# Value products of the last key block in one strided instruction, one softmax scaling on ScalarE, and five operations moved: a hybrid encoder layer on Trainium2

## The chip, the cores and the metric

The kernel runs on one core of one Trainium2 chip. The metric is the device time of one execution in microseconds (us). The engines are TensorE (PE: products; PEld: its weight loads), VectorE (DVE), ScalarE (ACT), GpSimd (POOL) and SyncE (SP), which issues most of the transfers; every engine works through its own instructions in order and waits on semaphores for the others.

## The reference, cut to what matters

One encoder layer over 512 positions of width 1024, all in float32:

```python
h = layer_norm(x, ln0_g, ln0_b)
mix = hybrid_mixer(h, ...)
h = layer_norm(DN_ALPHA * h + mix, ln1_g, ln1_b)
h = layer_norm(DN_ALPHA * h + sq_relu_mlp(h, w_ff1, w_ff2), ln2_g, ln2_b)

# hybrid_mixer(u):
proj = u @ w_in            # q, k, v | z, x, B, C, dt | two gates
ya = neighbourhood_attention(q, k, v, rpb) @ w_attn_br
ys = ...                   # two-way Mamba-2 SSD in 8 groups, gated norm, @ w_ssd_br
merged = gates[:, :, 0] * ya + gates[:, :, 1] * ys
return merged @ w_o
```

The neighbourhood attention sees the 512 positions as a grid of 8 rows by 64 columns. Each query looks at all 8 rows and at 16 columns around its own, with a bias by relative position: `softmax(q k' / 8 + bias) v` for 16 heads of width 64.

## The kernel before

**Products in parts.** A float32 product is made of three products of rounded parts: high by high, low by high, high by low (`mm3`, L398 to L401). The high part of a weight slab is a rounding copy on ScalarE (L381, or L504 in the planned stages), the low part a subtraction on VectorE or GpSimd (L382, L508). Products accumulate in PSUM banks that are shared by tags: `mm` 2, `tr` 2, `so` 2, `yd` 1, `cb` 1.

**Stages, in order of time.** First norm and first projections (to about 46 us), the eight SSD groups (to about 500 us), the projection of the values (L1179 to L1194), the attention of 16 heads in 8 pairs (L1217 to L1333), its output projection `ps_abr` (L1348 to L1379), the gates and the merge (L1402 to L1414), `w_o`, the two feed-forward products, and at the very end the last quarter of the second one with the last norm (L1720 to L1741).

**What sets the order.** Up to the end of the SSD groups the order is a list: the first operations stand in a table, `HEAD` (L72 to L103), the others come from `Plan.order`, which simulates the engines with the cost of each operation; `Plan.issue` (L341 to L349) issues them as they are listed. Everything behind that is ordered by the tile framework, which simulates the engines' time, and where an edit changes a cost or a dependence there, instructions of all engines move. `behind(a, b)` and `after=` add a dependence of order.

**Places the change touches.** (1) In the chain for `dts` (softplus of the step widths) ScalarE copies `dtT` (L671), takes an absolute value (L683), an Exp (L684) and a second Exp for `ea` (L685); the Exp table is loaded before the first Exp. (2) In SSD group g, chunk c, a decay matrix `bc{g}_{c}` arrives by a transfer; VectorE subtracts (L958), selects (L962), ScalarE takes the Exp (L964), VectorE multiplies by the chunk's `cb` (L966), and TensorE uses it for the diagonal products `yd` (L972). Four reductions of the diagonal of `cb` (L882, two instructions each) lie between. (3) GpSimd multiplies a gate by the SSD result `ysacc` (L1409), twice for each of four blocks of columns. (4) For one head the scores of 4 query blocks m against 256 keys each lie in `sc` (128 x 4 x 256). VectorE adds the bias and takes the maximum (L1279), ScalarE takes the Exp with sums (L1285), VectorE the reciprocal of the sums (L1287) and four scalings (L1289). TensorE transposes eight blocks of 128 columns (`tp_p`, L1300), ScalarE copies the high parts `pth` (L1304), VectorE subtracts the low parts `ptl` (L1305), and TensorE multiplies the values by them into `po` (L1313, L1314, bank `yd`, one for all heads). Key block b serves the two query blocks b and b+1 modulo 4: for b = 0, 1, 2 they lie side by side in `po` and one product has 256 columns; for b = 3 they are blocks 3 and 0, and each has a product of 128 columns. ScalarE then copies one half of `po` (`low`, L1324) and VectorE adds both into `aT` (L1327). (5) The split of the second weight slab of the output projection, `wh_abr1`, is held behind the last `aTh` (L1352). (6) In the last loop (L1720) each block of 128 positions gets two products of 512 columns, each followed by an addition (L1727) and statistics (L1728).

Of the kernel before, what the change touches and what calls it, by code (L numbers as in the profile page):

```python
# [19 lines left out]
P = 128  # L20
S = 512
D = 1024
# [69 lines left out]
T:ps_dt.1 T:ps_dt.1 T:ps_dt.1 T:ps_x0_2.0 A:dtT.0 T:ps_x0_3.0 T:ps_x0_3.0 T:tp_dt.0  # L92
T:ps_x0_0.0 D:dts.0 T:ps_x0_1.0 T:ps_x0_1.0 A:dts.1 T:ps_x0_0.1 A:dts.1 T:ps_x0_1.1
T:ps_x0_1.1 T:ps_x0_0.1 T:ps_x0_0.1 T:ps_x0_0.1 A:ea.0 D:dts.2 T:ps_x0_2.0 D:dts.2
# [9 lines left out]
ON = {x[2:]: x[0] for x in HEAD}  # L104


class Plan:
# [233 lines left out]
    def issue(self):  # L341
        order = self.order(NUDGES)
        named = {}
        for o in self.ops:
            named.setdefault(".".join(map(str, o["w"][0])), []).append(o["i"])
        head = [named[x[2:]].pop(0) for x in HEAD]
        done = set(head)
        for i in head + [i for i in order if i not in done]:
            self.ops[i]["fn"]()  # L349
# [3 lines left out]
def encoder_layer(ctx, tc, x, w_in, w_attn_br, w_ssd_br, w_o, w_ff1, w_ff2, pcols, rows64,  # L353
# [825 lines left out]
    for s in range(2):  # L1179
# [9 lines left out]
        for b in range(4):  # L1189
            pv4 = pss[b].rearrange("p (r h q) -> p r h q", r=4, h=2)  # L1190
            hi = vhl[s][:, b, :, 0:4:3, :]
            nc.scalar.activation(hi, pv4, AF.Copy)
            nc.vector.tensor_tensor(out=vhl[s][:, b, :, 1:3, :], in0=pv4, in1=hi.bitcast(F32),
                                    op=ALU.subtract)  # L1194
# [22 lines left out]
    for pr in range(NH // 2):  # L1217
# [25 lines left out]
        for hh in range(2):  # L1243
# [44 lines left out]
            for m in range(4):  # L1288
                nc.vector.tensor_scalar(out=sc[:, m, :], in0=sc[:, m, :], scalar1=sums[:, m : m + 1],  # L1289
                                        scalar2=None, op0=ALU.mult)  # L1290

            pts = []
            for b2 in range(2):
                tp = psx.tile([P, 2, 2, P], F32, tag="tr", bufs=BANKS["tr"], name=f"tp_p{h}_{b2}")
                for j in range(2):
                    b = 2 * b2 + j
                    for which in range(2):
                        m = (b + which) % 4
                        half = (0 if b == 0 else 1) if m == 0 else 1 - which
                        nc.tensor.transpose(tp[:, j, which, :],  # L1300
                                            sc[:, m, half * P : (half + 1) * P], ident)
                pth = atp.tile([P, 2, 2, P], F32R, tag="pth", bufs=3, name=f"pth{h}_{b2}")
                ptl = atp.tile([P, 2, 2, P], F32R, tag="ptl", bufs=3, name=f"ptl{h}_{b2}")
                nc.scalar.activation(pth, tp, AF.Copy)  # L1304
# [5 lines left out]
            def pv(b, w0, nw, m0, start, stop):  # L1310
                th, tl = (t[:, b % 2, w0 : w0 + nw, :] for t in pts[b // 2])
                v = vhl[pr // 4][:, b, pr % 4, 2 * hh : 2 * hh + 2, :]
                nc.tensor.matmul(po[:, m0 : m0 + nw, :], v, th, start=start, stop=False)  # L1313
                return nc.tensor.matmul(po[:, m0 : m0 + nw, :], v, tl, start=False, stop=stop)  # L1314


            pv(0, 0, 2, 0, True, False)
            pv(2, 0, 2, 2, False, False)
            pv(1, 0, 2, 1, False, False)
            pv(3, 0, 1, 3, False, False)  # L1320
            last = pv(3, 1, 1, 0, False, True)
# [27 lines left out]
    for d2 in range(4):  # L1349
        wa = weights([(w_attn_br, 0, d2 * 256, 256)], KD, 256, f"abr{d2}",  # L1350
                     nc.vector if d2 else nc.gpsimd,
                     after=(ins.ins, ins.ins) if d2 == 1 else None)  # L1352
# [49 lines left out]
    for d2 in range(4):  # L1402
# [3 lines left out]
        for j in range(2):  # L1406
            d = 2 * d2 + j
            g0, g1 = ga[:, j, :], gs[:, j, :]
            nc.gpsimd.tensor_tensor(out=g1, in0=g1, in1=ysacc[:, d, :], op=ALU.mult)  # L1409
# [310 lines left out]
    for t in range(NT):  # L1720
        st = ffp.tile([P, 2, 6], F32, tag="ln2_st", bufs=2, name=f"ln2_st{t}")
        for i, slab in enumerate(slabs):
            ps = psx.tile([P, 512], F32, tag="mm", bufs=BANKS["mm"], name=f"ps_f2_3_{t}_{i}")
            for k0, w2 in zip((0, 4), slab):
                ff2(ps, t, *w2, k0)
            cs = slice(i * 512, (i + 1) * 512)
            nc.vector.tensor_tensor(out=acc[t][:, cs], in0=ps, in1=acc[t][:, cs], op=ALU.add)  # L1727
            nc.vector.bn_stats(st[:, i, :], acc[t][:, cs])  # L1728
# [7 lines left out]

        ends = (0, 512, 768, D) if t == NT - 1 else (0, 512, D)
# [65 lines left out]
```

## Time and profile before

| | us |
|---|---|
| median of 3 runs | 1187.24 (1186.92 to 1188.7) |
| profiled execution, its own time | 1186.48 |
| span of the profiled execution | 1184.7 |
| TensorE busy | 1158.4 |
| VectorE busy | 757.0 |
| ScalarE busy | 614.7 |
| GpSimd busy | 546.6 |

The mean granted TensorE clock was 0.997 of full speed. Rows of a timeline give start, duration, engine, line, operation, output and inputs, shapes and the number of equal instructions in a row; in brackets stands how long the engine had been idle and what ended that. Matmuls are pipelined: their own durations overlap, and the time that one takes of TensorE is read from its start to the next start. A list of waits gives the time in total, how often, and the longest.

### The profile page before, as it was taken

The page shows a single profiled execution, that of the slowest core. Times are in us where ns is not written, and L with a number is a line of the kernel's source. Part 1 is how long each engine was busy: PE and PEld are TensorE (multiplying, and loading weights), DVE is VectorE, ACT ScalarE, POOL GpSimd, SP SyncE. Part 2 cuts the span into 40 slices and gives each one's busy share as a digit, 9 for nine tenths or more (in the row PEclk, how much of TensorE's full clock was granted, in tenths as well). Part 3 has the DMA queues.
Part 4 walks back from the last instruction along what each step waited for, and adds up shares of the span by engine and source line. Part 5 has one row for each costly group of instructions (what it writes and reads, how often), then busy time and mean ns, then how long its engine had stood idle before and what let it go on. Part 6 is the DMA issues. An engine that isn't in the chain of part 4 may idle for free.

```text
span 1184.7 us, 16407 instructions
## 1 busy us (share of the span) xinstructions
PE 1158.4 (98%) x6114; PEld 988.1 (83%) x6114; DVE 757.0 (64%) x1361; ACT 614.7 (52%) x1033; POOL 546.6 (46%) x588
## 2 busy tenths in 40 slices
PE   5999999999999999999999999999999999999997
PEld 5988798989888888788888887888888888878885
DVE  7747475666657656443789975556543557488855
ACT  6676583837354654423667864342353555365410
POOL 1268968777788776403567541016046131222000
PEclk9999999999999999999999999999999999999999
DMA  6343333333333331333333223444236977788511
GB/s 201 105 150 124 105 127 107 116 112 129 104 110 107 125 124 54 107 106 85 86 86 86 57 69 107 156 147 144 87 107 181 240 195 199 184 212 226 167 50 54
DMA packets 129407, 149.19 MB, mean 126 GB/s; under 512 B 22960, under 2 KB 101808, under 8 KB 129328
## 3 DMA queue, kind: packets, MB, share of 16 engines
q1 hardware_dynamic: 115696, 112.63, 30.9%
q0 software_dynamic: 13056, 34.61, 12.0%
q8 instruction: 48, 0.79, 0.3%
q10 hardware_dynamic: 576, 0.92, 0.2%
q14 instruction: 31, 0.25, 0.1%
HBM read 145.90 MB, written 2.23 MB: 125 GB/s over the span
## 4 chain that ended last, share of the span: by engine, by line
PE 90%; DVE 3%; DMA 3%; issue 1%; ACT 1%; POOL 1%; DVEq 0%; SPq 0%; POOLq 0%; ACTq 0%
PE ps_f L399 8%; PE ps_f L401 8%; PE ps_f L400 8%; PE ps_x L401 5%; PE ps_x L399 5%; PE ps_x L400 5%; PE ps_abr L1363 3%; PE ps_g L399 2%; PE ps_g L401 2%; PE ps_g L400 2%; PE ps_z L399 2%; PE ps_sbr L399 2%; PE ps_z L400 2%; PE ps_z L401 2%; PE ps_sbr L401 2%; PE yd L972 2%
## 5 line engine op out<-in xcount | busy, mean ns | idle before, releaser
L779 DVE SCALAR_TENSOR_TENSOR cv<-ps_x,pc,cv 128x511 f32<-128x511 f32 (+1 forms) x128 | 95.7, 748 | 24.9 <-ACT cv L771 21.3
L400 PE MATMUL ps_f<-h1Th,wl_f 128*128 128x512 f32 (+1 forms) x288 | 104.0, 365 | 0.0
L399 PE MATMUL ps_f<-h1Th,wh_f 128*128 128x512 f32 (+1 forms) x288 | 103.7, 365 | 0.0
L401 PE MATMUL ps_f<-h1Tl,wh_f 128*128 128x512 f32 (+1 forms) x288 | 102.0, 365 | 0.0
L1564 DVE TENSOR_TENSOR wl_f<-w2r,wh_f 128x1024 fp32r<-128x1024 f32 x42 | 50.0, 1221 | 62.9 <-ACT wh_f L1563 62.6
L399 PE MATMUL ps_z<-wh_z,hTh 128*128 128x256 f32 x256 | 75.2, 294 | 1.0 <-DVE cv L779 1.0
L401 PE MATMUL ps_z<-wl_z,hTh 128*128 128x256 f32 x256 | 71.5, 279 | 0.0
L400 PE MATMUL ps_z<-wh_z,hTl 128*128 128x256 f32 x256 | 71.5, 279 | 0.0
L1558 POOL DMA_DIRECT2D w2r<-in_w_ff x30 | 36.3, 1421 | 71.7 <-DMA w2r<-in_w_ff 46.6
L400 PE MATMUL ps_f<-wh_f,sql 128*128 128x512 f32 x168 | 65.3, 390 | 0.3 <-DVE sql L1564 0.3
L1563 ACT ACTIVATE wh_f<-w2r 128x1024 fp32r<-128x1024 f32 x42 | 42.7, 1053 | 43.6 <-DMA w2r<-in_w_ff 33.5
L401 PE MATMUL ps_f<-wl_f,sqh 128*128 128x512 f32 x168 | 65.2, 390 | 0.1
L399 PE MATMUL ps_f<-wh_f,sqh 128*128 128x512 f32 x168 | 64.9, 389 | 0.0
L1094 DVE TENSOR_TENSOR ysacc<-ps_sbr,ysacc 128x512 f32<-128x512 f32 x56 | 38.4, 689 | 39.2 <-PE ps_sbr L401 39.0
L399 PEld LDWEIGHTS ps_f<-h1Th,wh_f 128*128 128x128 f32 x288 | 53.9, 188 | 9.1 <-ACT rl L1665 0.2
L400 PEld LDWEIGHTS ps_f<-h1Th,wl_f 128*128 128x128 f32 x288 | 53.9, 188 | 8.7
L382 DVE TENSOR_TENSOR wl_f<-ws_f,wh_f 128x1024 fp32r<-128x1024 f32 x36 | 47.2, 1348 | 20.7 <-ACT wh_f L381 20.5
L401 PEld LDWEIGHTS ps_f<-h1Tl,wh_f 128*128 128x128 f32 x288 | 52.8, 188 | 8.7
L1409 POOL TENSOR_TENSOR gt<-gt,ysacc 128x512 f32<-128x512 f32 x8 | 13.1, 1651 | 99.2 <-ACT gt L1112 91.1
L399 PE MATMUL ps_sbr<-yTh,wh_sbr 128*128 128x512 f32 x128 | 55.5, 434 | 1.1 <-DVE ysacc L1094 0.6
L399 PE MATMUL ps_x<-hTh,wh_bc 128*128 128x512 f32 (+1 forms) x144 | 56.6, 393 | 0.0
L401 PE MATMUL ps_x<-hTl,wh_bc 128*128 128x512 f32 (+1 forms) x144 | 53.6, 372 | 1.8 <-DVE hTl L621 1.8
(344 smaller groups left out, 3766.2 us busy)
## 6 DMA issues: line engine op xcount, KB each, us to landing
ws_f<-in_w_ff SPq DMA_DIRECT2D x20, 1024.0 KB
w2r<-in_w_ff POOLq DMA_DIRECT2D x18, 1024.0 KB, 7.5
bc<-acs_d SPq DMA_DIRECT2D x32, 512.0 KB
w2r<-in_w_ff POOLq DMA_DIRECT2D x30, 512.0 KB, 9.1
ws_bc<-in_w_in SPq DMA_DIRECT2D x16, 512.0 KB
ws_x<-in_w_in SPq DMA_DIRECT2D x8, 1024.0 KB
ws_z<-in_w_in SPq DMA_DIRECT2D x8, 1024.0 KB
ws_g<-in_w_in SPq DMA_DIRECT2D x8, 1024.0 KB
```

The lines of the kernel that those rows point to most:

```text
L382: (eng[i] if isinstance(eng, tuple) else eng).tensor_tensor(out=lo[:, k], in0=st[:, k], in1=hi[:, k].bitcast(F32), op=ALU.subtract)
L399: nc.tensor.matmul(o, lh, rh, start=start, stop=False)
L400: nc.tensor.matmul(o, ll, rh, start=False, stop=False)
L401: return nc.tensor.matmul(o, lh, rl, start=False, stop=stop)
L779: op("DVE", 0.75, lambda j=j, o=o, n=n: nc.vector.scalar_tensor_tensor(out=acc()[:, o], in0=ps()[:, n], scalar=tap(j), in1=acc()[:, o], op ...
L972: nc.tensor.matmul(yd()[:, c % 2, h * HD : (h + 1) * HD], bc()[:, 1, h, :], xtok()[:, c, h * HD : (h + 1) * HD], start=True, stop=True)
L1094: op("DVE", 0.69, lambda d=d, ps=ps: nc.vector.tensor_tensor(out=ysacc[:, d, :], in0=ps(), in1=ysacc[:, d, :], op=ALU.add), r=[(ps.name, 0 ...
L1363: ins.append(nc.tensor.matmul(pss[j], u, v, start=k + p == 0, stop=k == KD - 1 and p == 2))
L1409: nc.gpsimd.tensor_tensor(out=g1, in0=g1, in1=ysacc[:, d, :], op=ALU.mult)
L1558: nc.gpsimd.dma_start(t, rows(i, n, c, k), accum_op=ALU.add)
L1563: nc.scalar.activation(hi[:, k], x, AF.Copy)
L1564: low = nc.vector.tensor_tensor(out=lo[:, k], in0=x, in1=hi[:, k].bitcast(F32), op=ALU.subtract)
```

## The change

Six edits. (a) In the table of the first operations the Exp for `ea`, and the table load with it, goes ahead of the copy `dtT`. (b) The product of `bc0_3` by `cb` goes ahead of the subtraction for `bc0_2`. (c) GpSimd's first two gate products wait for the last eviction of the values. (d) The scaling of query block 0 goes to ScalarE; the transposes of key block 3 are stored in swapped order, and its products become one per part, with 256 columns that go to blocks 0 and 3 of `po`. (e) The split of `wh_abr1` waits for the last `pth` instead of the last `aTh`. (f) The second 512 columns of the last block of positions are done in two halves.

```diff
-T:ps_dt.1 T:ps_dt.1 T:ps_dt.1 T:ps_x0_2.0 A:dtT.0 T:ps_x0_3.0 T:ps_x0_3.0 T:tp_dt.0
...
+T:ps_dt.1 T:ps_dt.1 T:ps_dt.1 T:ps_x0_2.0 A:ea.0 A:dtT.0 T:ps_x0_3.0 T:ps_x0_3.0
...
+MOVE = (("bc0_3.1", 2), ("bc0_2.0", 1))
...
+        early, late = (named[x][n] for x, n in MOVE)
         head = [named[x[2:]].pop(0) for x in HEAD]
+        order.remove(early)
+        order.insert(order.index(late), early)
...
-            nc.scalar.activation(hi, pv4, AF.Copy)
+            vdone = nc.scalar.activation(hi, pv4, AF.Copy)
...
             for m in range(4):
-                nc.vector.tensor_scalar(out=sc[:, m, :], in0=sc[:, m, :], scalar1=sums[:, m : m + 1],
-                                        scalar2=None, op0=ALU.mult)
+                if m == 0:
+                    nc.scalar.activation(sc[:, m, :], sc[:, m, :], AF.Copy, scale=sums[:, m : m + 1])
+                else:
+                    nc.vector.tensor_scalar(out=sc[:, m, :], in0=sc[:, m, :],
+                                            scalar1=sums[:, m : m + 1], scalar2=None, op0=ALU.mult)
...
-                        nc.tensor.transpose(tp[:, j, which, :],
+                        nc.tensor.transpose(tp[:, j, 1 - which if b == 3 else which, :],
...
-                nc.scalar.activation(pth, tp, AF.Copy)
+                high_t = nc.scalar.activation(pth, tp, AF.Copy)
...
-            def pv(b, w0, nw, m0, start, stop):
-                th, tl = (t[:, b % 2, w0 : w0 + nw, :] for t in pts[b // 2])
+            for i, (b, ms) in enumerate(((0, slice(0, 2)), (2, slice(2, 4)), (1, slice(1, 3)),
+                                         (3, slice(0, 4, 3)))):
                 v = vhl[pr // 4][:, b, pr % 4, 2 * hh : 2 * hh + 2, :]
-                nc.tensor.matmul(po[:, m0 : m0 + nw, :], v, th, start=start, stop=False)
-                return nc.tensor.matmul(po[:, m0 : m0 + nw, :], v, tl, start=False, stop=stop)
-            pv(0, 0, 2, 0, True, False)
-            pv(2, 0, 2, 2, False, False)
-            pv(1, 0, 2, 1, False, False)
-            pv(3, 0, 1, 3, False, False)
-            last = pv(3, 1, 1, 0, False, True)
+                for j, t in enumerate(pts[b // 2]):
+                    last = nc.tensor.matmul(po[:, ms, :], v, t[:, b % 2], start=i + j == 0,
+                                            stop=i == 3 and j == 1)
...
-                     after=(ins.ins, ins.ins) if d2 == 1 else None)
+                     after=(high_t.ins, high_t.ins) if d2 == 1 else None)
...
-            nc.gpsimd.tensor_tensor(out=g1, in0=g1, in1=ysacc[:, d, :], op=ALU.mult)
+            gy = nc.gpsimd.tensor_tensor(out=g1, in0=g1, in1=ysacc[:, d, :], op=ALU.mult)
+            if d2 == 0:
+                behind(gy, vdone, "the values")
...
+        ends = (0, 512, 768, D) if t == NT - 1 else (0, 512, D)
...
+        for i, (c0, c1) in enumerate(zip(ends, ends[1:])):
+            ps = psx.tile([P, c1 - c0], F32, tag="mm", bufs=BANKS["mm"], name=f"ps_f2_3_{t}_{i}")
...
+                ff2(ps, t, w2[0][:, :, cs], w2[1][:, :, cs], k0)
+            nc.vector.tensor_tensor(out=acc[t][:, c0:c1], in0=ps, in1=acc[t][:, c0:c1], op=ALU.add)
+            nc.vector.bn_stats(st[:, i, :], acc[t][:, c0:c1])
```

What that moves, at three places. In the listings a line number is that of the kernel listed, and a number behind a name tells one buffer from another.

VectorE in the first SSD group, around the chunks 2 and 3: before,

```order
L962 COPY_PREDICATED bc0_3_784<-msk_100,bc0_3_784 128x512
L958 TENSOR_TENSOR bc2_3_788<-bc2_3_788,amd_103 128x512
L958 TENSOR_TENSOR bc0_2_790<-bc0_2_790,amd_103 128x512
L882 ISA junk0_869,cbd0_870<-cb0_854,cst_81 128x128
L882 ISA cbd0_870 128x1
L966 TENSOR_TENSOR bc0_3_784<-bc0_3_784,cb0_854 128x512
L890 TENSOR_TENSOR coef0_894<-dt_102,cbd0_870 128x16
```

and with the change

```order
L967 COPY_PREDICATED bc0_3_784<-msk_100,bc0_3_784 128x512
L963 TENSOR_TENSOR bc2_3_788<-bc2_3_788,amd_103 128x512
L971 TENSOR_TENSOR bc0_3_784<-bc0_3_784,cb0_854 128x512
L963 TENSOR_TENSOR bc0_2_790<-bc0_2_790,amd_103 128x512
L887 ISA junk0_870,cbd0_871<-cb0_854,cst_81 128x128
L887 ISA cbd0_871 128x1
L895 TENSOR_TENSOR coef0_894<-dt_102,cbd0_871 128x16
```

The pair of L882 (L887) stands there four times. The product by `cb` has moved ahead of the subtraction for `bc0_2` and of the four pairs.

ScalarE at the end of the attention (heads 14 and 15): before,

```order
L1324 ACTIVATE low13_6684<-po13_6673 64x512
L1304 ACTIVATE pth14_1_6839<-tp_p14_1_6834 128x512
L1215 ACTIVATE aTh_5951<-aT_4690 128x512
L1304 ACTIVATE pth15_0_6907<-tp_p15_0_6902 128x512
L1324 ACTIVATE low14_6854<-po14_6843 64x512
L1304 ACTIVATE pth15_1_6916<-tp_p15_1_6911 128x512
L1324 ACTIVATE low15_6931<-po15_6920 64x512
L1112 ACT_TABLE_LOAD
L1112 ACTIVATE gt1_1_7009<-ps_g2_1_7010,pc_83 128x512
L1112 ACTIVATE gt1_1_7009<-ps_g3_1_7036,pc_83 128x512
L381 ACTIVATE wh_abr1_7136<-ws_abr1_7138 128x1024 x2
```

and with the change

```order
L1290 ACTIVATE sc15_6845,sums15_6847<-sc15_6845,mx15_6846 128x256 x4
L1295 ACTIVATE sc15_6845<-sc15_6845,sums15_6847 128x256
L1328 ACTIVATE low13_6656<-po13_6647 64x512
L1313 ACTIVATE pth14_1_6811<-tp_p14_1_6806 128x512
L1220 ACTIVATE aTh_5935<-aT_4690 128x512
L1313 ACTIVATE pth15_0_6877<-tp_p15_0_6872 128x512
L1328 ACTIVATE low14_6824<-po14_6815 64x512
L1313 ACTIVATE pth15_1_6886<-tp_p15_1_6881 128x512
L386 ACTIVATE wh_abr1_7104<-ws_abr1_7106 128x1024 x2
L1328 ACTIVATE low15_6899<-po15_6890 64x512
```

The scaling (L1295) stands between the Exps of its head and the next eviction, and the split of `wh_abr1` has moved ahead of `low15`, the table load and the sigmoids; before, the last `aTh` stood ahead of it too.

TensorE at the end of the attention: before,

```order
L1313 MATMUL po14_6843<-pth14_1_6839,vhl1_4695 128x128
L1314 MATMUL po14_6843<-ptl14_1_6840,vhl1_4695 128x128
L1300 MATMUL tp_p15_1_6911<-cst_81,sc15_6875 128x128 x4
L1363 MATMUL ps_abr1_7085<-aTh_5951,wl_abr0_7077 128x512
L1363 MATMUL ps_abr1_7085<-aTh_5951,wh_abr0_7076 128x512
L1313 MATMUL po15_6920<-pth15_0_6907,vhl1_4695 128x256
```

and with the change

```order
L1324 MATMUL po14_6815<-pth14_1_6811,vhl1_4695 128x2x128
L1324 MATMUL po14_6815<-ptl14_1_6812,vhl1_4695 128x2x128
L1309 MATMUL tp_p15_1_6881<-cst_81,sc15_6845 128x128 x4
L1324 MATMUL po15_6890<-pth15_0_6877,vhl1_4695 128x256
L1324 MATMUL po15_6890<-ptl15_0_6878,vhl1_4695 128x256
L1324 MATMUL po15_6890<-pth15_1_6886,vhl1_4695 128x256
L1367 MATMUL ps_abr2_7112<-aTh_5935,wh_abr1_7104 128x512
L1324 MATMUL po15_6890<-ptl15_1_6887,vhl1_4695 128x256
```

Before, nine `ps_abr1` products stood between the transposes and the first value product of head 15 (the two rows in turn, five and four times). With the change none stands there, and the first product with `wh_abr1` comes between head 15's third and fourth value product.

## Rows read from the trace of the kernel before

**Rows 1.** The page: the busy time of each engine with its share of the span and its instructions, and the chain of work that ended last, by engine.

```profile
PE 1158.4 (98%) x6114; PEld 988.1 (83%) x6114; DVE 757.0 (64%) x1361; ACT 614.7 (52%) x1033; POOL 546.6 (46%) x588
...
PE 90%; DVE 3%; DMA 3%; issue 1%; ACT 1%; POOL 1%; DVEq 0%; SPq 0%; POOLq 0%; ACTq 0%
```

**Rows 2.** What TensorE's products waited for over the whole run: product and line, what ended the wait, us in total, times, longest.

```profile
PE ps_abr L1363 <- DVE wl_abr L382: 0.9, 1, 0.9
PE ps_q L399 <- ACT qf L1223: 0.8, 1, 0.8
PE yd L972 <- issue: 0.7, 1, 0.7
PE ps_sbr L399 <- DVE ysacc L1094: 0.6, 1, 0.6
...
PE po L1313 <- ACT qf L1223: 0.3, 1, 0.3
```

**Rows 3.** ScalarE's timeline, 29 to 36 us.

```profile
31.86 0.59 ACT L671 ACTIVATE dtT<-ps_dt 64x512 f32<-64x512 f32 x1 [1.38 <-PE ps_dt L401]
...
34.16 1.28 ACT L684 ACT_TABLE_LOAD   x1
```

**Rows 4.** VectorE's timeline, 73.5 to 79.5 us.

```profile
76.28 0.69 DVE L958 TENSOR_TENSOR bc<-bc,amd 128x512 f32<-128x512 f32 x1 [0.61 <-DMA bc<-acs_d]
76.89 0.28 DVE L882 CUSTOM_DVE_ANT_0 junk<-cb,cst 128x128 f32<-128x128 f32 x1
...
78.10 0.68 DVE L966 TENSOR_TENSOR bc<-bc,cb 128x512 f32<-128x512 f32 x1
```

**Rows 5.** TensorE's timeline, 77 to 79.6 us.

```profile
77.78 0.40 PE L401 MATMUL ps_x<-hTl,wh_bc 128*128 128x512 f32 x1
78.88 0.96 PE L972 MATMUL yd<-xtok,bc 128*128 128x64 f32 x7 [0.70 <-issue]
```

**Rows 6.** TensorE's timeline, 707.5 to 711 us: the end of head 14's value products (the four of 128 columns from 707.82 on), the last transposes of head 15, nine products of ps_abr (the first and the last) and head 15's first value product.

```profile
707.70 0.28 PE L1314 MATMUL po<-ptl,vhl 128*128 128x256 f32 x1
707.82 0.22 PE L1313 MATMUL po<-pth,vhl 128*128 128x128 f32 x1
707.88 0.27 PE L1314 MATMUL po<-ptl,vhl 128*128 128x128 f32 x1
...
708.10 0.28 PE L1314 MATMUL po<-ptl,vhl 128*128 128x128 f32 x1
708.21 0.62 PE L1300 MATMUL tp_p<-cst,sc 128*128 128x128 f32 x4
708.59 0.48 PE L1363 MATMUL ps_abr<-aTh,wl_abr 128*128 128x512 f32 x1
...
710.50 0.39 PE L1363 MATMUL ps_abr<-aTh,wl_abr 128*128 128x512 f32 x1
710.73 0.28 PE L1313 MATMUL po<-pth,vhl 128*128 128x256 f32 x1
```

**Rows 7.** GpSimd's timeline, 488 to 562 us.

```profile
493.77 4.37 POOL L1409 TENSOR_TENSOR gt<-gt,ysacc 128x512 f32<-128x512 f32 x2 [8.10 <-DVE ysacc L1094]
...
552.18 0.46 POOL L1257 TENSOR_TENSOR bias<-raw,cst 128x128 f32<-128x128 f32 x1 [4.21 <-DMA raw<-in_rpb_pad]
```

**Rows 8.** VectorE's timeline, 492 to 499 us.

```profile
493.54 1.22 DVE L382 TENSOR_TENSOR wl_v<-ws_v,wh_v 128x1024 fp32r<-128x1024 f32 x1
...
495.27 1.72 DVE L382 TENSOR_TENSOR wl_v<-ws_v,wh_v 128x1024 fp32r<-128x1024 f32 x1
```

**Rows 9.** The scalings of line 1289: durations in ns as least, median and most, first and last start; and who waited for them (us, times).

```profile
L1289 DVE TENSOR_SCALAR sc<-sc,sums x64: 341/355/1451, 569.1 to 704.3; 128x256 f32<-128x256 f32 x64
...
  PEld tp_p L1300: 0.5, 2
```

**Rows 10.** ScalarE's timeline, 588 to 591 us: the Exps of one head, the first, and the reading of the last one's sum.

```profile
588.51 0.49 ACT L1285 ACTIVATE sc<-sc,mx 128x256 f32<-128x256 f32 x1
...
590.39 0.19 ACT L1285 ACTIVATION_READ_ACCUMULATOR sc<-sc,mx 128x1 f32 x1
```

**Rows 11.** VectorE's timeline, 595 to 596 us: the reciprocal of the same head.

```profile
595.11 0.18 DVE L1287 RECIPROCAL sums<-sums 128x4 f32<-128x4 f32 x1
```

**Rows 12.** ScalarE's timeline, 707 to 716.5 us.

```profile
709.09 0.60 ACT L1304 ACTIVATE pth<-tp_p 128x512 fp32r<-128x512 f32 x1
...
715.67 1.05 ACT L381 ACTIVATE wh_abr<-ws_abr 128x1024 fp32r<-128x1024 f32 x1
```

**Rows 13.** VectorE's timeline, 708 to 711 us.

```profile
709.10 0.94 DVE L1327 TENSOR_TENSOR aT<-po,low 64x128 f32<-64x128 f32 x5 [0.41 <-ACT low L1324]
```

**Rows 14.** The chain that ended last, 1175 to 1186 us, in order of time: start, us, what. L1727 and L1728 handle 512 columns; of the two pieces of L1739 shown the first is one of 512 columns, the second of 256.

```profile
1176.41 0.70 DVE acc L1727
...
1177.13 0.70 DVE ln_st L1728
...
1180.14 0.75 DVE acc L1739
...
1181.28 0.40 DVE acc L1739
```

**Rows 15.** VectorE's timeline, 635 to 637 us.

```profile
635.23 0.99 DVE L1327 TENSOR_TENSOR aT<-po,low 64x128 f32<-64x128 f32 x5
```

**Rows 16.** TensorE's timeline, 635 to 637 us.

```profile
636.37 0.36 PE L1313 MATMUL po<-pth,vhl 128*128 128x256 f32 x1 [0.35 <-ACT qf L1223]
```

More of the change, by code (lines that the diff above doesn't have):

```diff
@@ L91 @@
 T:ps_x0_3.0 A:hmb1_6.0 T:ps_dt.1 A:hmb1_7.0 T:ps_dt.1 D:hTl.6.1 T:ps_dt.1 D:hTl.7.1
-T:ps_dt.1 T:ps_dt.1 T:ps_dt.1 T:ps_x0_2.0 A:dtT.0 T:ps_x0_3.0 T:ps_x0_3.0 T:tp_dt.0
-T:ps_x0_0.0 D:dts.0 T:ps_x0_1.0 T:ps_x0_1.0 A:dts.1 T:ps_x0_0.1 A:dts.1 T:ps_x0_1.1
-T:ps_x0_1.1 T:ps_x0_0.1 T:ps_x0_0.1 T:ps_x0_0.1 A:ea.0 D:dts.2 T:ps_x0_2.0 D:dts.2
+T:ps_dt.1 T:ps_dt.1 T:ps_dt.1 T:ps_x0_2.0 A:ea.0 A:dtT.0 T:ps_x0_3.0 T:ps_x0_3.0
+T:tp_dt.0 T:ps_x0_0.0 D:dts.0 T:ps_x0_1.0 T:ps_x0_1.0 A:dts.1 T:ps_x0_0.1 A:dts.1
+T:ps_x0_1.1 T:ps_x0_1.1 T:ps_x0_0.1 T:ps_x0_0.1 T:ps_x0_0.1 D:dts.2 T:ps_x0_2.0 D:dts.2
 T:ps_x0_1.1 T:ps_x0_2.0 T:ps_x0_0.1 T:ps_x0_0.1 T:ps_x0_2.0 D:dts.3 T:ps_x0_1.1
@@ L1720, in encoder_layer @@
     for t in range(NT):
[L1721 to L1728, printed above, removed]
+        ends = (0, 512, 768, D) if t == NT - 1 else (0, 512, D)
+        st = ffp.tile([P, len(ends) - 1, 6], F32, tag=f"ln2_st{len(ends)}", bufs=2, name=f"ln2_st{t}")
+        for i, (c0, c1) in enumerate(zip(ends, ends[1:])):
+            ps = psx.tile([P, c1 - c0], F32, tag="mm", bufs=BANKS["mm"], name=f"ps_f2_3_{t}_{i}")
+            cs = slice(c0 % 512, c0 % 512 + c1 - c0)
+            for k0, w2 in zip((0, 4), slabs[c0 // 512]):
+                ff2(ps, t, w2[0][:, :, cs], w2[1][:, :, cs], k0)
+            nc.vector.tensor_tensor(out=acc[t][:, c0:c1], in0=ps, in1=acc[t][:, c0:c1], op=ALU.add)
+            nc.vector.bn_stats(st[:, i, :], acc[t][:, c0:c1])
         mv = ffp.tile([P, 2], F32, tag="ln2_mv", bufs=2, name=f"ln2_mv{t}")
@@ L1735, in encoder_layer @@
                                            in1=row2[0][:, cs], op0=ALU.subtract, op1=ALU.mult)
-        ends = (0, 512, 768, D) if t == NT - 1 else (0, 512, D)
         for i, (c0, c1) in enumerate(zip(ends, ends[1:])):
```

## The prediction, made before the changed kernel had run

> **What bounds the kernel now.** I read the page's busy times and chain first: TensorE is busy 98% of the span and holds 90% of the chain that ended last [rows 1], so an edit pays only where it shortens TensorE's own work or a moment in which TensorE stands. Such moments are read next, from the list of what TensorE waited for [rows 2]: they are short, and four of them lie at places that the diff touches (the diagonal products yd of the first group, the branch products ps_sbr, the projection ps_q and the value products po of the attention, and ps_abr). Then I read the timelines around these places, one engine at a time, and the end of the chain.
>
> **The change part by part.** A measurement of this kernel tells about 0.2% (2.4 us) from no change. Every edit below is smaller than that or about as large, so only the sum decides.
>
> *The Exp of `ea` ahead of `dtT`.* The Exp table's load of 1.28 us stands between two operations of the `dts` chain now; ScalarE was idle 1.38 us before `dtT` [rows 3], so the load fits there and the short `ea` nearly. `dtT` comes one or two tenths later, the chain behind it about 1.1 us earlier. TensorE has no wait on this chain in the list [rows 2]: I take 0, bounds -0.3 to +0.2.
>
> *The mask product of `bc0_3`.* VectorE is idle 0.61 us for the transfer of `bc0_2` (until 76.28), then does that subtraction and four diagonal reductions, and only at 78.10 the product that yd needs [rows 4]. TensorE's last product before it starts at 77.78 and yd at 78.88, 0.70 us of it idle [rows 2, 5]; a 512-column product's start to the next start is 0.23 [rows 6], so 1.10 - 0.23 = 0.87 us is lost. Put into the idle time, the product is 1.8 us earlier and the wait goes. Late next would be the transfer's subtraction, pushed back by 0.1 us, which feeds the next yd. I take -0.8 (bounds -0.9 and 0: all of it may be given back at a later wait).
>
> *The gate product on GpSimd.* It runs from 493.77 for 4.37 us [rows 7], and beside it VectorE's second `wl_v` split takes 1.72 us, the first 1.22 [rows 8]. TensorE then waits 0.6 us for the `ysacc` behind that split [rows 2]. Gone from there, the split is back at 1.22: -0.5 (bounds -0.75 and 0). The two products now stand behind the last value eviction, where GpSimd was idle 4.21 us for the transfer of `raw` [rows 7]. If they take the whole 4.37 us again, `bias` is late by at most about 1 us and is not needed by a score product but by the VectorE step after it: 0.
>
> *Two pairs of products become one.* In a head, four products of 128 columns take from 707.82 to 708.21, 0.39 us; one of 256 columns takes 0.12 from start to start [rows 6]. Two of 256 take 0.24, so each of 16 heads saves 0.15: -2.4 us, all on TensorE. That a short product costs nearly as much as a long one is what the row shows (0.06 to 0.11 against 0.12). No row has a product with a strided output; bounds are -2.4 (it costs as any 256-column product does) and 0 (twice that); I take -2.4, since the row of the same length is the nearest. By the Trainium skill (TensorE: Matmul & The Clock Gate, Back-to-back issue gap) an isolated product takes N/2.4 ns plus 2.5 ns; worked out from that page, four of 128 would take 0.223 us and two of 256 0.218, and the term would be an estimated -0.1 instead of -2.4. The row above, with 0.39, disagrees.
>
> *One scaling of four on ScalarE.* VectorE loses 16 of 64 scalings (median 0.36, at most 1.45 us [rows 9]); ScalarE gets 16 of about 0.5 us, by the Exp of the same tile [rows 10]. The scaling needs the reciprocal, which VectorE usually delivers within 0.3 us of the last Exp; in the head with Exps from 588.51 it came at 595.11, with the Exps over at 590.58 [rows 10, 11]. ScalarE runs in order, so pth, low and the rest stand behind that wait. Before, TensorE's transposes waited for the scalings twice in 16 heads, 0.5 us in all [rows 9], so there is room for a scaling that takes 0.15 longer, and three others that come one place earlier. I take 0; bounds: -0.7 (of the attention's waits, 0.8 for ps_q and 0.3 for po [rows 2], most goes) to +2.4 (every head's first transposes come 0.15 us later, 0.5 against 0.36). The Trainium skill (ScalarE: Activation LUTs, Rules for kernel authors) speaks against this edit: it puts a multiply on VectorE. By the same page (What ACT_TABLE_LOAD costs) an ACTIVATE with one per-partition pointer operand is an estimated 186 + 93 + 0.833 x 256 = 492 ns, with which the trace agrees by the Exp's 0.49; if nothing covered the difference the sum would be some 2 us worse by it.
>
> *The split of `wh_abr1` and the end of the attention.* The split stands at 715.67 behind a table load, two sigmoids and `aTh` [rows 12], and TensorE waits 0.9 us for what follows from it [rows 2]. It now follows `pth15_1` directly: -0.9. But TensorE's order changes too. Before, nine ps_abr products (708.59 to 710.73) stand between head 15's transposes and its first value product [rows 6]; now none does. The value products of all heads share one PSUM bank, and head 15 may not start before head 14's sums have left it. Head 14's last value product is done near 708.21; `low` follows on ScalarE, and `aT` on VectorE ends at 709.10 + 0.94 = 710.04 [rows 13]. That is 1.83 us, of which the four transposes fill 0.38 [rows 6]: TensorE stands 1.45 us. Three products later it wants `wh_abr1`: `pth15_1` ends at 709.69 [rows 12], the half split 1.05 later, at 710.74, against 710.04 + 3 x 0.12 = 710.40: another 0.34. Together +1.45 + 0.34 - 0.9 = +0.9 (bounds -0.9, if the earlier heads' lead shortens these chains, and +1.8, if the old wait stays).
>
> *The last 512 columns in two halves.* After the last product, add and statistics of 512 columns take 0.70 each. A 256-column pass takes 0.40 where a 512-column one takes 0.75 [rows 14]. The first half runs beside the second half's products, so 2 x 0.3 is saved, less 0.15 for 24 more, shorter products: -0.45 (bounds -0.6 and 0).
>
> Sum: 0 - 0.8 - 0.5 - 2.4 + 0 + 0.9 - 0.45 = -3.25 us. The profiled execution took 1186.48, 0.76 below the median of the runs shown, 1187.24; its own time would become 1183.2. Against the median the forecast is **1184.0 us**.
>
> **The rivals.**
>
> *The drain of a head's bank falls behind the new wait (slower).* `low`, which frees the bank of the value products, stands in several heads directly behind the new scaling on ScalarE, and that behind VectorE's reciprocal. Before, the next head's first value product came little after `aT` was done in five heads: 0.15 us in the first of them, head 5 (done at 635.23 + 0.99, started at 636.37 [rows 15, 16]), 0.69 in the last, head 14 (710.04 to 710.73 [rows 6, 13]), 2.71 in all five. Where ScalarE comes late by d in each of them, and d is over every spare, they cost 5d - 2.71. At the 0.5 of the scaling alone little shows; at d = 1.67 they cost 5.65 and the kernel is slower by 2.4; at 1.8 they cost 6.3: 1184.0 + 6.3 = 1190.3. The late reciprocal of rows 11 speaks for it (4.5 us after its Exps), against it that this happened in three heads of sixteen and that VectorE has less to do. Chance 0.13.
>
> *The merged products gain nothing.* A strided output may cost twice, or the short products may cost half a long one as soon as others stand around them: the first of the four starts 0.06 before the second [rows 6], and 4 x 0.06 is no more than 2 x 0.12. The term is 0 instead of -2.4 and the time 1186.4. The rows of 0.39 speak against the second form, nothing speaks for or against the first. The second form is what the Trainium skill's page on TensorE, above, comes to. Chance 0.10.
>
> *The early gains are given back.* The two waits taken away at 78 and 497 us are followed by others on VectorE and on transfers; if each is found again at the next one, the -1.3 of both goes and the time is 1185.3. Against it: TensorE leads the chain nearly everywhere [rows 1]. Chance 0.20.
>
> **How the numbers follow.** The forecast has 0.57. Its own spread, from the bounds of the terms (all at their better ends: -0.3 - 0.9 - 0.75 - 2.4 - 0.7 - 0.9 - 0.6 = -6.5), reaches to about 1181 with some likelihood; upwards the second and third rival reach to 1186.4, and with most of the scaling's +2.4 not hidden to 1188.2. 1181.0 to 1188.2 leaves out the first rival and little else. Faster by over 0.2% means below 1184.87: nearly nine tenths of the forecast (0.50) and a third of the given-back case (0.07): 0.57. Slower is the first rival: 0.13. The rest, 0.30, is within 0.2%.
>
> **What would show it.** In the profile after: no wait of yd on "issue"; the second `wl_v` at about 1.22; eight value products a head, the last two 0.12 apart; a wait of 1.4 us of head 15's first value product on `aT`, and none of ps_abr on `wl_abr`; add and statistics of about 0.4 behind the last product. Two products with a strided output that take 0.24 from start to start would break the largest term; new waits of po or tp_p on ScalarE in many heads would bring the first rival.

## The result, and the profile after

The changed kernel is slower: a median of 1191.62 us (1189.76 to 1193.54, 6 runs) beside 1187.08 (1185.61 to 1188.7, 6 runs) for the kernel before in the same comparison, a ratio of 1.0044, 95% interval 1.0034 to 1.0055. The forecast was 1184.0, range 1181.0 to 1188.2. The profiled execution of after took 1190.74, its span is 1189.0, 4.3 more than before's.

The page of after, against [rows 1]. The slice of PEclk that shows an 8 is the 24th of 40, about 684 to 713 us: the end of the attention.

```profile
PE 1159.4 (98%) x6106; PEld 990.1 (83%) x6106; DVE 758.6 (64%) x1347; ACT 620.6 (52%) x1049; POOL 546.6 (46%) x588
...
PEclk9999999999999999999999989999999999999999
```

What TensorE's products waited for in after, against [rows 2] (product and line, what ended the wait, us in total, times, longest). Line numbers of after are about 5 higher: `pss` (L1279, L1280) are the score products, VectorE's bias and maximum stand in L1284, the scalings in L1295 (ScalarE) and L1297 (VectorE), `po` in L1324.

```profile
PE pss L1279 <- DVE mx L1284: 3.4, 1, 3.4
PE ps_q L404 <- ACT qf L1228: 2.6, 2, 1.4
...
PE po L1324 <- DVE aT L1331: 1.4, 1, 1.4
```

The waits of `yd`, of `ps_sbr` on `ysacc`, of `ps_abr` and of `po` on `qf` are gone, as the forecast had it for the first three. A wait of 3.4 us has come that it did not have, at 693 us. VectorE around it (head 13's scalings behind two bias steps of head 14):

```profile
690.29 0.42 DVE L1284 CUSTOM_DVE_ANT_0 sc<-pss,bias 128x256 f32<-128x256 f32 x1
...
690.63 5.57 DVE L1297 TENSOR_SCALAR sc<-sc,sums 128x256 f32<-128x256 f32 x3
696.12 0.41 DVE L1284 CUSTOM_DVE_ANT_0 sc<-pss,bias 128x256 f32<-128x256 f32 x1
696.46 0.08 DVE L1284 DVE_READ_ACCUMULATOR2_ANT mx<- 128x1 f32 x1
696.46 0.41 DVE L1284 CUSTOM_DVE_ANT_0 sc<-pss,bias 128x256 f32<-128x256 f32 x1
```

GpSimd in the same stretch, the low parts of `wl_abr0`:

```profile
691.32 4.73 POOL L387 TENSOR_TENSOR wl_abr<-ws_abr,wh_abr 128x1024 fp32r<-128x1024 f32 x2
```

TensorE:

```profile
693.17 0.39 PE L405 MATMUL ps_g<-hTh,wl_g 128*128 128x512 f32 x1
696.94 0.58 PE L1279 MATMUL pss<-kh,qs 128*128 128x256 f32 x1 [3.38 <-DVE mx L1284]
...
699.47 0.58 PE L1324 MATMUL po<-ptl,vhl 128*128 128x256 f32 x1
699.85 0.41 PE L1324 MATMUL po<-pth,vhl 128*128 128x256 f32 x1
700.07 0.41 PE L1324 MATMUL po<-ptl,vhl 128*128 128x256 f32 x1
```

and the busy time of the engines by stretch (behind the stretch's length stand the busy time and count of TensorE, its weight loads, VectorE, ScalarE and GpSimd, then the granted clock of TensorE as a share of full speed; the last two numbers are of transfers):

```profile
690.00:694.00 4.00, 3.56 (x18) 2.70 (x16) 4.00 (x8) 3.22 (x5) 3.92 (x3) 1.00 0.00 0
694.00:697.00 3.00, 0.06 (x1) 0.06 (x1) 3.00 (x6) 0.00 (x0) 2.09 (x2) 0.85 0.00 0
697.00:700.00 3.00, 3.00 (x12) 2.64 (x13) 2.34 (x8) 1.47 (x5) 2.06 (x4) 0.50 0.95 324
700.00:703.00 3.00, 3.00 (x13) 2.77 (x12) 1.80 (x9) 2.71 (x9) 0.00 (x0) 0.51 0.07 26
703.00:706.00 3.00, 3.00 (x15) 2.49 (x14) 2.75 (x12) 0.82 (x3) 0.00 (x0) 1.00 0.00 0
```

Two other heads' scalings, for comparison, the first beside GpSimd instructions of 0.46, 0.51 and 1.29 us, the second with nothing of GpSimd beside them:

```profile
650.87 2.37 DVE L1297 TENSOR_SCALAR sc<-sc,sums 128x256 f32<-128x256 f32 x3
...
679.51 0.88 DVE L1297 TENSOR_SCALAR sc<-sc,sums 128x256 f32<-128x256 f32 x3
```

Read together: three scalings that take 0.88 us alone take 5.57, for as long as GpSimd works. The next score products of TensorE need the bank that the bias step of L1284 empties; it is queued behind the scalings and comes at 696.12, and TensorE stands. When it goes on, the granted clock is 0.50 (1.2 GHz): products of 256 columns stand 0.21 us apart instead of 0.12. From 696.94 to 703.00 TensorE does 12 products of 256 columns, 8 transposes and 3 products of 512: 12 x 0.12 + 8 x 0.11 + 3 x 0.23 = 3.0 us at full clock. It took 6.06. The place costs 3.5 us of standing and 3.1 of half clock.

The whole loss lies in the attention. From the first `ps_q` product to the last `ps_abr` product, both by their starts, before took 204.24 us and after 210.19. The difference of 5.95, read from the distance of each product's start to the next, waits as far as they are over the usual distance (0.23 us behind a product of 512 columns, 0.12 behind one of 256, 0.11 behind a transpose, 0.10 behind a value product of 128):

| attention stage | us |
|---|---|
| the value products of key block 3, 0.395 to 0.239 in each of 16 heads | -2.50 |
| standing at 693 us | +3.54 |
| half clock behind it | +3.07 |
| waits of `ps_q` on `qf`, one of 0.92 to two of 2.93 | +2.01 |
| head 15's first value product on its bank | +1.54 |
| waits of before that are gone (`ps_abr` 1.05, `po` on `qf` 0.52) | -1.57 |
| smaller differences | -0.14 |
| sum | +5.95 |

The rest of the 4.3: the stage began 1.2 us earlier, the end behind the last product is 0.6 shorter, and between the two 0.1 was lost.

The other places of the forecast. VectorE in the first SSD group, against [rows 4]: the product (L971) now stands in the idle time.

```profile
75.06 0.69 DVE L963 TENSOR_TENSOR bc<-bc,amd 128x512 f32<-128x512 f32 x1 [0.82 <-DMA bc<-acs_d]
75.67 0.68 DVE L971 TENSOR_TENSOR bc<-bc,cb 128x512 f32<-128x512 f32 x1
76.37 0.84 DVE L963 TENSOR_TENSOR bc<-bc,amd 128x512 f32<-128x512 f32 x1
```

TensorE there, against [rows 5], and its last value products of one head and head 15's start, against [rows 6]:

```profile
78.08 0.40 PE L406 MATMUL ps_x<-hTl,wh_bc 128*128 128x512 f32 x1
78.31 1.00 PE L977 MATMUL yd<-xtok,bc 128*128 128x64 f32 x8
...
685.67 0.27 PE L1324 MATMUL po<-ptl,vhl 128*128 128x256 f32 x1
685.78 0.28 PE L1324 MATMUL po<-pth,vhl 128*128 128x256 f32 x1
685.90 0.28 PE L1324 MATMUL po<-ptl,vhl 128*128 128x256 f32 x1
686.02 0.60 PE L1309 MATMUL tp_p<-cst,sc 128*128 128x128 f32 x4
...
714.67 0.60 PE L1309 MATMUL tp_p<-cst,sc 128*128 128x128 f32 x4
716.64 0.36 PE L1324 MATMUL po<-pth,vhl 128*128 128x256 f32 x1 [1.37 <-DVE aT L1331]
```

GpSimd's gate products in their new place, against [rows 7]; VectorE's second `wl_v` split, against [rows 8], is at 1.22:

```profile
548.10 3.28 POOL L1413 TENSOR_TENSOR gt<-gt,ysacc 128x512 f32<-128x512 f32 x2 [1.31 <-ACT vhl L1197]
```

```profile
494.60 1.22 DVE L387 TENSOR_TENSOR wl_v<-ws_v,wh_v 128x1024 fp32r<-128x1024 f32 x1
```

The scalings, VectorE's and ScalarE's, against [rows 9] (least, median, most in ns), and the first steps behind the last product, against [rows 14]:

```profile
L1297 DVE TENSOR_SCALAR sc<-sc,sums x48: 340/394/2542, 568.0 to 708.6; 128x256 f32<-128x256 f32 x48
```

```profile
L1295 ACT ACTIVATE sc<-sc,sums x16: 493/502/512, 568.0 to 708.1; 128x256 f32<-128x256 f32 x16
```

```profile
1181.19 0.43 DVE acc L1735
...
1181.65 0.44 DVE ln_st L1736
```

### The profile page after: what moved, and what is told of

It reads as the page before. It is cut to its first block, busy times and chain, and to the rows that moved or that the text cites. A ratio compares the mean times of both kernels' runs of the same rounds, so it can differ in the third digit from the quotient of the medians.

```text
span 1189.0 us, 16379 instructions
## 1 busy us (share of the span) xinstructions
PE 1159.4 (98%) x6106; PEld 990.1 (83%) x6106; DVE 758.6 (64%) x1347; ACT 620.6 (52%) x1049; POOL 546.6 (46%) x588
## 4 chain that ended last, share of the span: by engine, by line
PE 37%; issue 4%; POOL 4%; DVE 3%; ACT 2%; DMA 2%; SPq 0%; POOLq 0%; DVEq 0%
PE ps_f L404 7%; PE ps_f L406 7%; PE ps_f L405 7%; PE ps_abr L1367 4%; PE ps_g L406 2%; PE ps_g L404 2%; PE ps_g L405 2%; DMA w2r<-in_w_ff 2%; POOL acc L1694 2%; PE ps_o L406 1%; PE ps_o L405 1%; PE ps_o L404 1%; DVE sc L1297 1%; ACT sc L1290 1%; PE po L1324 1%
```

## The experiments

Nine kernels ran, in three groups of four, three and two; the kernel before ran beside each group (medians 1186.74, 1186.03, 1186.65). The letters are those of the change: a `ea`, b the mask product, c the gate products, d the scaling on ScalarE together with the merged products, e the split of `wh_abr1`, f the last halves; where (d) is taken apart, "scaling" and "merged" say which. The stage is measured as above, in the one profiled execution. The ratios are those on record and not quotients of the medians shown.

| kernel | us | ratio to before | stage, us |
|---|---|---|---|
| before | 1187.08 | 1 | 204.24 |
| after | 1191.62 | 1.0044 (1.0034 to 1.0055) | 210.19 |
| after, head 13's scalings in another form | 1191.26 | 1.0037 (1.0025 to 1.0049) | 210.15 |
| after without the scaling on ScalarE | 1196.57 | 1.0072 (1.0059 to 1.0085) | 213.92 |
| after without the merged products | 1186.2 | 1.0 (0.9989 to 1.001) | 205.77 |
| after without e | 1192.96 | 1.0044 (1.003 to 1.0057) | 210.43 |
| after, GpSimd's split held back | 1191.41 | 1.0045 (1.0031 to 1.0059) | 208.54 |
| after, GpSimd's split in pieces | 1187.68 | 1.0014 (1.0005 to 1.0024) | 205.99 |
| a, b, c, f alone | 1185.78 | 0.9995 (0.9987 to 1.0004) | 204.30 |
| merged products alone | 1198.3 | 1.01 (1.0087 to 1.0113) | 215.80 |
| scaling on ScalarE alone | 1190.51 | 1.0031 (1.0019 to 1.0044) | 206.93 |

Where the stage's order is the same its time repeats: 204.24 and 204.30 in before and in a, b, c, f alone, 210.19 and 210.15 in after and in after with the other form. The whole time varies more: the profiled execution is the slowest of its kernel's runs in after without e (1195.79) and in the merged products alone (1200.04).

**Head 13's three scalings on VectorE in another form.**

```diff
+                elif h == 13:
+                    nc.vector.tensor_tensor(out=sc[:, m, :], in0=sc[:, m, :],
+                                            in1=sums[:, m : m + 1].to_broadcast([P, 256]), op=ALU.mult)
```

> The changed kernel, but head 13's three VectorE scalings are written as a product of two tensors (the reciprocal broadcast along the row) instead of a scaling by a per-partition scalar; the order of all engines stays that of the change. Theory 1 (GpSimd's split of wl_abr0 holds that form of instruction: the three took 5.57 us while it ran 4.73): the three take about 0.42 each, 1.3 us in all; TensorE's wait of 3.4 us for head 14's scores goes, the stretch at half clock behind it too, and the time falls by about 6 us to 1185.5 (1184.5 to 1187). Rival 2 (ScalarE late by the wait for the reciprocal): nothing changes, 1191.6. Rival 3 (the merged products cost more than they save): 1191.6.

The three took 5.87 us beside a split of 4.95, and the wait of 3.4 stayed. So it is not the form of the operation that makes it stand beside GpSimd.

```profile
691.27 5.87 DVE L1297 TENSOR_TENSOR sc<-sc,sums 128x256 f32<-128x256 f32 x3
```

**Without the scaling on ScalarE.**

```diff
             for m in range(4):
-                if m == 0:
-                    nc.scalar.activation(sc[:, m, :], sc[:, m, :], AF.Copy, scale=sums[:, m : m + 1])
-                else:
-                    nc.vector.tensor_scalar(...)
+                nc.vector.tensor_scalar(out=sc[:, m, :], in0=sc[:, m, :], scalar1=sums[:, m : m + 1],
+                                        scalar2=None, op0=ALU.mult)
```

> The changed kernel with all four scalings of a head on VectorE again; the framework orders the attention anew. Theory 1: what counts is whether scalings meet the GpSimd split of wl_abr0; if head 13's four do, 1190 or more, with a scaling of several us in the trace; if they don't, 1185 to 1187. Rival 2 (the wait of ScalarE's scaling for the reciprocal is the loss): without that wait 1184 to 1186, whatever GpSimd does.

It is slower still: stage 213.92. Head 13's four scalings take 5.45 us beside the same split, now in front of the transposes, which wait 2.9 for `ptl`, and the clock falls to 0.54 between 703 and 706 us. Beside the merged products the scaling on ScalarE is no cause of the loss: it gives 3.7 us of the stage back.

**Without the merged products.**

```diff
-                        nc.tensor.transpose(tp[:, j, 1 - which if b == 3 else which, :],
+                        nc.tensor.transpose(tp[:, j, which, :],
...
-                    last = nc.tensor.matmul(po[:, ms, :], v, t[:, b % 2], ...)
+            pv(3, 0, 1, 3, False, False)
+            last = pv(3, 1, 1, 0, False, True)
```

> The changed kernel with the four products of 128 columns a head instead of the two merged ones; ordered anew. Theory 1: 2.4 us more for the products; if no scaling stands beside the GpSimd split in this order, 6 us less for that wait: 1188 (1186 to 1189.5); if one does, 1194. Rival 3 (the strided output costs): below 1188 even where a scaling stands beside the split. Rival 2: 1194, since the scaling on ScalarE stays.

Level with before. VectorE does head 13's scalings at 687 us and GpSimd's split follows at 690:

```profile
687.14 1.30 DVE L1297 TENSOR_SCALAR sc<-sc,sums 128x256 f32<-128x256 f32 x3
```

```profile
690.50 4.74 POOL L387 TENSOR_TENSOR wl_abr<-ws_abr,wh_abr 128x1024 fp32r<-128x1024 f32 x2 [2.21 <-ACT wh_abr L386]
```

The value products of key block 3 take 0.395 us a head again, where after has 0.239, which is 2.50 us over 16 heads: the merged products do save what was forecast, and lose it by where they put the other engines' work. Head 15's wait for its bank (1.4 us) is here as well.

**The split of `wh_abr1` behind the last `aTh` again.**

```diff
-                     after=(high_t.ins, high_t.ins) if d2 == 1 else None)
+                     after=(ins.ins, ins.ins) if d2 == 1 else None)
```

> The changed kernel with the split of wh_abr1 held behind the last aTh again. The order up to head 14 is the changed kernel's, so theory 1 expects the long scalings of head 13 and the 3.4 us wait to stay. The wait for wl_abr1 of about 0.9 us comes back, and the wait of head 15's first value product of 1.4 us stays if it is the bank's and goes if it came with the new place of the split. 1191.6 to 1192.5 in the first case, 1191 in the second.

The wait of `ps_abr` is back (1.0), the stage is 0.24 longer, and the waits of 3.4 and of 1.4 at head 15 stay. The stretch at half clock is shorter than in after (granted clock 0.60 from 701 to 704 us and 0.83 from 704 to 707, work from 701.26 on): it costs 1.8 us where after's cost 3.1, which hides 1.2 us of what the edit gains in the stage. The bank wait that the forecast charged to this edit is not the edit's.

**GpSimd's split behind head 13's last scaling.**

```diff
+            if name == "abr0":
+                behind(lo_ins, scaled[13], "head 13's weights")
...
+                    scaled[h] = nc.vector.tensor_scalar(...)
```

> The changed kernel with one dependence more: GpSimd's split of wl_abr0 waits for head 13's last VectorE scaling. The order of every engine is the changed kernel's. Theory 1, mended by the run with the other form of instruction (any VectorE operation between SBUF tensors takes turns with a GpSimd instruction, whatever its form): the three scalings take about 1 us instead of 5.57, the wait of 3.4 us before head 14's scores and the 6 us at half clock behind it go, -6 us against the changed kernel: 1185.5 (1184.5 to 1187). If VectorE was late there for another reason, 1191.5.

The scalings are short again and the wait of 3.4 is gone, but the time is not better. The split starts at 691.73, and now the next VectorE operations between SBUF tiles stand beside it:

```profile
690.29 1.27 DVE L1301 TENSOR_SCALAR sc<-sc,sums 128x256 f32<-128x256 f32 x3
...
692.17 2.50 DVE L1351 TENSOR_TENSOR aTl_kf<-aT,aTh 128x512 fp32r<-128x512 f32 x1
694.68 0.99 DVE L1336 TENSOR_TENSOR aT<-po,low 64x128 f32<-64x128 f32 x5
695.71 1.20 DVE L1292 TENSOR_SCALAR mx<-mx 128x4 f32<-128x4 f32 x1
```

`aTl_kf` takes 2.50 us where it takes 0.69 otherwise, even the scaling of 4 columns 1.20; `aT` between them, which reads PSUM, keeps its 0.99. TensorE stands 2.0 and 1.4 us between 693.7 and 697.7, and the clock is at 0.53 from 697 to 700. The victim changed, the meeting stayed. (The profiled execution is the fastest of six; its stage of 208.54 goes with 1188.69, not with the median.)

**GpSimd's split in eight pieces of 256 columns.**

```diff
-            (eng[i] if isinstance(eng, tuple) else eng).tensor_tensor(out=lo[:, k], ...)
+            for k1 in range(k.start, k.stop) if name == "abr0" else (k,):
+                (eng[i] if isinstance(eng, tuple) else eng).tensor_tensor(
+                    out=lo[:, k1], in0=st[:, k1], in1=hi[:, k1].bitcast(F32), op=ALU.subtract)
```

> The changed kernel with GpSimd's split of wl_abr0 in eight pieces of 256 columns instead of two of 1024; order otherwise the changed kernel's. If a VectorE scaling waits for one GpSimd instruction in turn, it waits 0.6 us instead of 2.4, three take 2 to 2.6 us, and most of the wait of 3.4 us goes: 1186 (1185 to 1188). If GpSimd's whole work holds VectorE, however it is cut, the three take 5 us or more again: 1191 to 1192.

The same meeting, in smaller steps:

```profile
690.35 2.33 DVE L1298 TENSOR_SCALAR sc<-sc,sums 128x256 f32<-128x256 f32 x3
...
693.29 1.23 DVE L1347 TENSOR_TENSOR aTl_kf<-aT,aTh 128x512 fp32r<-128x512 f32 x1
```

```profile
691.04 6.12 POOL L388 TENSOR_TENSOR wl_abr<-ws_abr,wh_abr 128x256 fp32r<-128x256 f32 x8
```

The scalings take 2.33 us instead of 5.57, the wait of 3.4 is gone, the clock stays at 1.00, and 4.2 of the stage's 5.95 us come back; the ratio to before falls from 1.0044 to 1.0014. GpSimd does no less work, nor at another time: it is the length of one GpSimd instruction that a VectorE operation has to sit out. What remains are the two `ps_q` waits (2.6) and two waits of `po` for `aT` (2.5).

**The edits a, b, c and f alone,** the attention as before.

> Only the edits outside the attention: the Exp of ea, the mask product of bc0_3, the gate product on GpSimd, the last columns in two halves; the attention is the kernel before's, in its order. From the traces so far the products begin the attention about 1.2 us earlier and the tail is 0.6 us shorter: -1.8 us, 1185.0 (1184.3 to 1185.8). If the early gains are given back, 1186 to 1186.7.

Not to be told from before; the expected 1185.0 lies inside the interval, the forecast's sum for these edits, -1.75 against before, just outside (its lower end is -1.5). The profiled executions show a spread that could cover it: in the eight kernels with b and c the stage's first product starts anywhere between 544.70 and 549.87 us, in the three without (before and the two below) between 546.73 and 549.03. This spread is larger than the gain.

**The merged products alone,** put into before.

> The kernel before with the merged products alone; the framework orders the attention as in the run without the scaling on ScalarE (head 13's four scalings next to GpSimd's split). Theory 1 (the new order, with scalings beside the split, is the loss, and the merged products set that order off): 2.4 us less of products, but some 9 us of waits as in that run, 1195 (1193 to 1197). If the merged products are worth what they save and the loss needs the scaling or the later split as well: 1183 to 1185.

The slowest of all. What it moves can be read in one row each of VectorE and GpSimd, and in TensorE's wait:

```profile
697.78 5.44 DVE L1289 TENSOR_SCALAR sc<-sc,sums 128x256 f32<-128x256 f32 x4
```

```profile
698.04 4.77 POOL L382 TENSOR_TENSOR wl_abr<-ws_abr,wh_abr 128x1024 fp32r<-128x1024 f32 x2
```

```profile
PE tp_p L1300 <- DVE ptl L1305: 3.6, 3, 2.8
```

TensorE's value products save 2.5 us as in after, and the stage is 11.6 longer all the same, so standing and half clock add 14.1 on balance: 3.0 at this place, 1.8 at 690 us, some ten smaller waits (head 15's for its bank, 1.5, among them), and 1.6 of half clock (0.62 from 706 to 709).

**The scaling on ScalarE alone,** put into before.

> The kernel before with one scaling of four on ScalarE alone. Theory 1: in this order the scalings of head 13 stand ahead of GpSimd's split or beside it depending on a fraction of a us; if ahead, the time stays within 2 us of 1186 (the run without the merged products, 1186.2, has this order too, with the early edits); if beside, 1189 or more. Rival 2 (ScalarE's wait for the reciprocal is the loss): 1189 or more, with waits of po on low and aT in many heads.

Slower by 0.2 to 0.4%. Two waits have come, `po` on `pth` at 694 us (0.7) and head 15's `po` on `aT` (1.4): the bank wait comes with this edit, without the split of `wh_abr1` and without merged products, as it came above with the merged products alone.

## Why the prediction was wrong, step by step

**Merged products, -2.4: right where they stand.** Products of 256 columns with a strided output stand 0.12 apart, and the last key block's products fell from 0.395 to 0.239 us a head: 2.50 us. The formula of the Trainium skill (TensorE: Matmul & The Clock Gate, Back-to-back issue gap), by which the saving would have been an estimated 0.1, does not give this; the same section says of it that it under-counts small products in a stream of weight loads and products.

**What failed is the step from there to the time.** The sum took each edit at its own instructions, and read a new order at the end of the attention alone. It was known that the framework orders this stage and moves instructions of all engines when a cost changes; but the term of the merged products was "all on TensorE", as if the other engines stayed where they were. They did not. With the merged products alone the stage is 11.6 us longer than before's, with all six edits 5.95, with everything but the merged products 1.5.

**The mechanism at the dearest place, shown by the runs.** A VectorE operation between SBUF tiles and a GpSimd instruction with two inputs take turns, one whole instruction at a time. Inside the row of 5.57 us the three scalings take 0.75, 2.54 and 2.42, the two GpSimd instructions 2.39 and 2.40. Another form changes nothing, shorter GpSimd instructions change it as their length does, a shift of GpSimd moves it to the next operation. The other heads of after show it in smaller doses: a scaling takes 0.35 us with no GpSimd instruction beside it, 0.5 to 0.6 beside one of about 0.5, and 1.42 to 1.45 beside one of 1.29. It holds the other way round too: GpSimd's bias step of 0.46 takes 1.44 us at 603.95, beside VectorE's subtraction `wl_qk` of 1.48 (from 603.58). Operations with a PSUM input are not held: beside the split held back, 0.41 for the bias step and 0.99 for `aT`. The Trainium skill (SBUF — State Buffer, Who interferes with whom) states this as a lock of the shared ports for the whole instruction, by a VectorE operation with two SBUF inputs or in a two-port mode; the trace agrees for operations with two SBUF inputs (`aTl_kf`, 0.69 to 2.50), and in which mode the scalings ran no run shows. And before showed it: the 1451 ns among the scalings of [rows 9] is one that began at 599.56, inside the first row, and GpSimd's row is the second:

```profile
598.30 2.72 DVE L1289 TENSOR_SCALAR sc<-sc,sums 128x256 f32<-128x256 f32 x4
```

```profile
599.57 1.29 POOL L1241 TENSOR_TENSOR klz<-kf,kh 64x512 fp32r<-64x512 f32 x1
```

The prediction used that number as the most a scaling takes, and did not ask what stood beside it. It knew the effect from [rows 7, 8], where a gate product holds a `wl_v` split, and priced it only at the place that the diff names. In before GpSimd's split of `wl_abr0` ran at 691.14 for 4.75 us too, but VectorE then had bias steps and `ptl`, which read PSUM; one small scaling took 1.05.

```profile
691.14 4.75 POOL L382 TENSOR_TENSOR wl_abr<-ws_abr,wh_abr 128x1024 fp32r<-128x1024 f32 x2 [3.05 <-issue]
```

```profile
691.35 0.42 DVE L1279 CUSTOM_DVE_ANT_0 sc<-pss,bias 128x256 f32<-128x256 f32 x1
...
692.50 1.05 DVE L1283 TENSOR_SCALAR mx<-mx 128x4 f32<-128x4 f32 x1
693.47 0.68 DVE L1305 TENSOR_TENSOR ptl<-tp_p,pth 128x512 fp32r<-128x512 f32 x1
```

**Half clock, not in the sum at all.** 3.1 us in after, so that a wait of 3.5 us cost 6.6. The price is not fixed: in after without e the same wait was followed by 1.8.

**Scaling on ScalarE, 0 (bounds -0.7 to +2.4): no single number holds for it.** Alone it costs 2.7 us of the stage (206.93 against 204.24); 1.5 of that is head 15's bank wait, which the forecast had counted at the end of the attention, and the other 1.2 lie inside the bounds. Beside the merged products it brings 3.7, outside them (213.92 to 210.19). It depends on the order around it.

**End of the attention, +0.9: the time of the wait right, its cause wrong.** Head 15 stands 1.37 us for `aT` (forecast 1.45), and `ps_abr` does not wait. But the bank wait is in the kernels without this edit too, and each half of (d) brings it alone. The edit itself takes away the wait of `ps_abr`, 1.1 us by the products' distances; in the stage only 0.24 of it shows, since the half clock lasted longer in after's profiled execution. The further 0.34 that the forecast added for `wh_abr1` did not come.

**Mask product -0.8, gate product -0.5: right where they stand. Last halves, -0.45: too large.** The `yd` products come 0.84 us earlier against the products before them, and the split is back at 1.22. Behind the last product's start the kernel is 0.6 us shorter (8.73 to 8.11), but the last 512 columns' products take 0.42 more (5.21 to 5.63, first start to last), where the forecast had 0.15: 0.20 us is left, in every kernel with f. The kernel with a, b, c and f alone gains 0.25 us (interval of the change -1.5 to +0.5) of the 1.75 forecast. That fits the third rival, which this interval does not settle: in after, of the 0.84 at 78 us 0.32 are lost again by 97 us.

**The rivals.** The one that ended slower had the side and the time (1190.3) but not the mechanism: `po` waits for `aT` once, not in five heads. The merged products gained where they stand, so the rival that gave them nothing is refuted. No rival had a meeting of VectorE and GpSimd.

**Open.** Why the framework's planned times put head 13's scalings beside GpSimd's split was not traced: they rest on its own costs, which no run here shows. The two `ps_q` waits (+2.0) come with the merged products and the scaling together; what orders them so was not tried. No version that beats before was found: the best are level with it. A kernel with the merged products in which GpSimd's split meets nothing of VectorE's was not run, so what they are worth then stays open; the split in pieces only shortens the meeting.

## What to carry to other kernels

Where a scheduler orders the work, an edit's cost is not that of its own instructions: list what moved on every engine for the whole stage, and look first for VectorE operations between SBUF tiles that now stand beside long GpSimd instructions. A duration in a list whose most is four times its median is a warning to follow: see what ran beside it before using the median. Short GpSimd instructions are a cheap protection, as the split in pieces shows (4.2 of 5.95 us came back, for 1.4 us more of GpSimd's time).

## What the runs showed of the hardware that was not expected

- A VectorE operation between SBUF tiles, of the forms that met one here, sits out one GpSimd instruction, whatever its own length: 0.35 us became 2.54, 0.69 became 2.50, a scaling of 4 columns went from 0.17 to 1.20.
- After TensorE had stood 3.5 us its granted clock was 0.50 for about 6 us of work in after, though it then worked without a break, and for about 3.4 us behind the same wait in after without e. Two waits of 2.0 and 1.4 us with a few products between had the same effect (0.53), waits of 1.3 and 0.5 in the kernel with GpSimd's split in pieces, and single ones of 1.5 there, had none.
- A product of 256 columns whose output goes to two separate blocks of PSUM takes the same 0.12 us as one with a contiguous output.
